# First blocks, attention and spatial gate of a streaming encoder step, with other tiles, engines and transposes

## Chip, cores and metric

One core of a Trainium2 chip runs the kernel. The metric is the device time of one execution in microseconds, the median of several runs.

## Reference

One layer of an encoder for two groups that share the weights: a prompt of 256 positions and a sample of 64 positions with 256 cached ones, 2048 features, 8 heads of 128, 8 spatial groups of 128, a feed-forward width of 5632. All in 32-bit floats. Cut to what matters:

```python
xn = rmsnorm(x, norm_mix)
q, k, v, u, vs, g = split(xn @ w_in)
# attention, for each head and query, keys in order:
z = (q . k) * 128 ** -0.5
mask = k_pos < q_pos
log_stay = where(mask, log_sigmoid(-z), 0)
log_rest = cumsum(log_stay, reverse=True) - log_stay
w = where(mask, exp(log_sigmoid(z) + log_rest), 0)
a = w @ v                       # sample: cached keys and values ahead of the new ones
# spatial gate, chunks of 128 positions, 8 groups:
vs = rmsnorm(gelu(vs), sgu_norm)
bb = gelu(u) * (w_spatial_masked @ vs + b_spatial)
h = x + (g_a * (a @ w_branch_a) + g_b * (bb @ w_branch_b)) @ w_out   # g_a, g_b: sigmoids of g
h = h + (silu(hn @ w_gate) * (hn @ w_up)) @ w_down                   # hn = rmsnorm(h)
y = rmsnorm(h)                  # and the new k, v and vs rows
```

## The kernel before

Features lie on partitions and the 320 positions of both groups side by side on the free axis. A 32-bit product is made of three matmuls in the reduced format fp32r: weight and activation are each split in a high and a low part, and `product` (lines 77 to 82) issues high x high (L80), high x low (L81), low x high (L82), each 128x128 by 320 columns. `block` (L84) makes one output block of 128 features from 16 k-chunks in two halves of 8. For each half `weights` (L67) lets the SP queue load 512 KB into one of three `raw` buffers, ScalarE cast it to `wh` (L72) and VectorE subtract to get `wl` (L73); four split buffers exist. Behind each half `tick` (L61) runs the steps that `at` has put at that count. A half is 24 matmuls.

The first stage computes q, k and v of heads 0 and 1 in six accumulators at once, two k-chunks a step, loads of x and weights alternating on the SP queue. Its norm `rms` (L156: one matmul by ones, square root, reciprocal, a Newton step) follows; behind one half `first_out` scales the six accumulators (L369, L372). Then heads 2 to 7 follow, three blocks each.

Attention goes by pairs of heads: `att_scores` (keys on rows; the sample's queries in strips), softplus by Abs, Exp, Ln on ScalarE and a sum on VectorE (L301 to L304), a split in two parts (L305, L306), `att_sums` (twelve matmuls by triangular and full matrices of -1, L317 to L322), `turned` (transposes of V on TensorE, L334) and `att_out` for each head (L357 to L360). `attend` (L381) sets their places: 2, 4, 6, 9 and 10 halves behind a pair's end. The spatial gate works the same way group by group (`sgu_turn`, `sgu_mix`, L419 to L436) between the blocks of u. Each engine runs its own instructions in program order, so a cast or a subtraction of weights waits for what stands ahead of it in its engine's queue. The ScalarE functions Exp and Ln need their tables loaded at each change between them.

## Time and profile before

| | |
|---|---|
| runs (us) | 1741.28, 1743.64, 1743.3; median 1743.3 |
| span of the profiled execution (us) | 1739.3 |
| TensorE (PE) busy | 1719.8 us, 99%, 11,672 instructions |
| VectorE (DVE) busy | 857.6 us, 49% |
| ScalarE (ACT) busy | 677.3 us, 39% |
| GpSimd (POOL) busy | 55.8 us, 3% |
| DMA | 263.20 MB, mean 151 GB/s |
| granted TensorE clock | 0.994 of full speed on average |

The span runs from the first to the last instruction of one profiled execution; the timed runs contain a little more around it. Busy shares are averages over the whole span. The chain that ended last lies on TensorE for 96% of the span, on the three lines of `product` for 31% each. A matmul's row gives its start and how long it was in the array; consecutive matmuls overlap, so the distance of starts tells what one costs.

### The profile page before, as it was taken

To read this page: it belongs to the slowest core of one execution; us is meant where nothing else is said; L and a number is where in the kernel's file an instruction comes from. 1 tells how busy PE (TensorE), PEld (TensorE's weight loads), DVE (VectorE), ACT (ScalarE), POOL (GpSimd) and SP (SyncE) were. 2 spreads that over 40 slices of the span, in tenths; PEclk is the share of its full clock that TensorE was granted. 3 is DMA by queue.
4 is the path that set the end of the run, shared out by engine and by line. 5 is a ranking of instruction groups with operands and counts; after the bars stand their busy time and mean duration, and the time that the engine had idled before them with its cause. 6 is when DMAs were issued, how large, how long until landed. Compare 5 with 4: busy or idle time off the path is not lost.

```text
span 1739.3 us, 27593 instructions
## 1 busy us (share of the span) xinstructions
PE 1719.8 (99%) x11672; PEld 1711.9 (98%) x11672; DVE 857.6 (49%) x1089; ACT 677.3 (39%) x832; POOL 55.8 (3%) x94
## 2 busy tenths in 40 slices
PE   9999999999999999999999999999999999999997
PEld 9999999999999999999999999999999999999996
DVE  6554446554444444555444444444444444444455
ACT  6554475333333333444333333233333323333342
POOL 1100001000000000220000000000000000000000
PEclk9999999999999999999999999999999999999998
DMA  7644434344444444554444444444444444444453
GB/s 215 200 155 161 142 119 151 122 146 147 154 148 148 155 146 155 175 172 149 154 146 149 154 146 150 153 145 151 152 147 152 150 148 153 148 148 153 129 152 109
DMA packets 80172, 263.20 MB, mean 151 GB/s; under 512 B 9008, under 2 KB 16432, under 8 KB 80048
## 3 DMA queue, kind: packets, MB, share of 16 engines
q1 hardware_dynamic: 77184, 252.74, 44.8%
q0 software_dynamic: 2720, 8.65, 1.5%
q8 instruction: 91, 1.49, 0.3%
q14 instruction: 33, 0.27, 0.0%
q10 hardware_dynamic: 144, 0.05, 0.0%
HBM read 255.90 MB, written 5.51 MB: 150 GB/s over the span
## 4 chain that ended last, share of the span: by engine, by line
PE 96%; DMA 2%; DVE 1%; ACT 1%; issue 0%; SPq 0%; DVEq 0%; ACTq 0%
PE acc L82 31%; PE acc L81 31%; PE acc L80 31%; DMA raw<-w_in 1%; ACT wh L72 0%; DVE wl L73 0%; PE aux L357 0%; DVE h L541 0%; DMA x<-xT 0%; PE aux L285 0%; PE aux L334 0%; PE aux L359 0%; PE aux L281 0%; PE aux L430 0%; PE aux L429 0%
## 5 line engine op out<-in xcount | busy, mean ns | idle before, releaser
L72 ACT CAST wh<-raw 128x1024 fp32r<-128x1024 f32 (+2 forms) x486 | 498.1, 1025 | 991.1 <-PE acc L81 802.1
L73 DVE TENSOR_TENSOR wl<-raw,wh 128x1024 fp32r<-128x1024 f32 (+2 forms) x486 | 580.6, 1195 | 527.7 <-ACT wh L72 527.3
L80 PE MATMUL acc<-A,wh 128*128 128x320 f32 x2496 | 775.6, 311 | 5.4 <-DVE q L369 3.4
L82 PE MATMUL acc<-A,wl 128*128 128x320 f32 x2496 | 772.7, 310 | 0.0
L81 PE MATMUL acc<-A,wh 128*128 128x320 f32 x2496 | 772.5, 309 | 0.0
L80 PEld LDWEIGHTS acc<-A,wh 128*128 128x128 f32 x2496 | 469.5, 188 | 6.5 <-issue 3.6
L82 PEld LDWEIGHTS acc<-A,wl 128*128 128x128 f32 x2496 | 469.6, 188 | 0.6 <-DVE wl L73 0.5
L81 PEld LDWEIGHTS acc<-A,wh 128*128 128x128 f32 x2496 | 469.7, 188 | 0.2
L82 PE MATMUL acc<-B,wl 128*128 128x320 f32 x960 | 296.6, 309 | 0.0
L80 PE MATMUL acc<-B,wh 128*128 128x320 f32 x960 | 296.6, 309 | 0.0
L81 PE MATMUL acc<-B,wh 128*128 128x320 f32 x960 | 296.6, 309 | 0.0
L80 PEld LDWEIGHTS acc<-B,wh 128*128 128x128 f32 x960 | 180.2, 188 | 0.0
L81 PEld LDWEIGHTS acc<-B,wh 128*128 128x128 f32 x960 | 180.2, 188 | 0.0
L82 PEld LDWEIGHTS acc<-B,wl 128*128 128x128 f32 x960 | 180.2, 188 | 0.0
L80 PE MATMUL acc<-mh,wh 128*128 128x320 f32 x256 | 79.1, 309 | 0.0
L81 PE MATMUL acc<-ml,wh 128*128 128x320 f32 x256 | 79.1, 309 | 0.0
L82 PE MATMUL acc<-mh,wl 128*128 128x320 f32 x256 | 79.1, 309 | 0.0
L503 DVE TENSOR_TENSOR bb<-acc,rh 128x320 f32<-128x320 f32 x44 | 21.6, 491 | 57.8 <-PE acc L82 57.8
L500 DVE TENSOR_TENSOR ev<-acc,rh 128x320 f32<-128x320 f32 x44 | 21.6, 491 | 56.6 <-PE acc L82 56.6
L513 DVE TENSOR_TENSOR h<-acc,h 128x320 f32<-128x320 f32 x48 | 23.5, 489 | 49.9 <-PE acc L82 49.9
L80 PEld LDWEIGHTS acc<-mh,wh 128*128 128x128 f32 x256 | 48.1, 188 | 0.0
L81 PEld LDWEIGHTS acc<-ml,wh 128*128 128x128 f32 x256 | 48.1, 188 | 0.0
(200 smaller groups left out, 761.2 us busy)
## 6 DMA issues: line engine op xcount, KB each, us to landing
raw<-w_gu SPq DMA_DIRECT2D x176, 512.0 KB, 3.5
raw<-w_in SPq DMA_DIRECT2D x132, 512.0 KB, 3.6
raw<-w_down SPq DMA_DIRECT2D x80, 512.0 KB, 3.5
raw<-w_out SPq DMA_DIRECT2D x32, 512.0 KB, 3.6
raw<-w_a SPq DMA_DIRECT2D x16, 512.0 KB, 3.5
raw<-w_b SPq DMA_DIRECT2D x16, 512.0 KB, 3.5
raw<-w_in SPq DMA_DIRECT2D x14, 384.0 KB, 5.0
raw<-w_down SPq DMA_DIRECT2D x16, 256.0 KB, 2.7
```

Of the source, the lines that this page charges most:

```text
L72: nc.scalar.copy(out=wh[:, : n * P], in_=raw[:, : n * P])
L73: nc.vector.tensor_tensor(out=wl[:, : n * P], in0=raw[:, : n * P], in1=wh[:, : n * P].bitcast(F32), op=ALU.subtract)
L80: nc.tensor.matmul(ps[:, :T], a, x[0], start=first, stop=False)
L81: nc.tensor.matmul(ps[:, :T], a, x[1], start=False, stop=False)
L82: nc.tensor.matmul(ps[:, :T], b, x[0], start=False, stop=last)
L500: nc.vector.tensor_tensor(out=t, in0=pg, in1=got["rh"], op=ALU.mult)
L503: nc.vector.tensor_tensor(out=u, in0=pu, in1=got["rh"], op=ALU.mult)
L513: nc.vector.tensor_tensor(out=hs[m], in0=ps, in1=hs[m], op=ALU.add)
```

## The change

First stage: ten raw buffers of its own (`raw1`), x loaded by pairs of chunks and some pairs ahead (`ahead`), squares by pairs; the norm's matmul stands before the last step's products; the six accumulators are scaled at once behind the stage. Attention: the two heads of a pair are handled together, queries on rows. The sample's queries of both heads share a tile (`qs`, 64 columns a head), and the products with cached keys and values fill 64 of 128 output rows each. The reverse cumulative sum is a scan on VectorE, five a pair (L311). The weights, V and the gate's input are transposed as two 16-bit planes: ScalarE copies a plane (L266, L267, L323), a transposing DMA on ScalarE's queue turns it (L269, L324), VectorE copies it back into 32-bit words (L277, L331). `att_out` makes both heads' prompt rows, and the sample's rows are transposed on TensorE from a copy (`own`). The spatial gate goes by pairs of groups, with a block-diagonal matrix `wd` for the sample. The activations' pairs of tiles come from one pool of 24 (before: 8 and a second pool). Nine warming matmuls instead of eight. The three lines of `product` are L82 to L84 now, cast and subtraction L69 and L70. A cut of the diff; lines taken out are seen in the functions above:

```diff
+    steps = [(0, 1), (1, 1)] + [(c, 2) for c in range(2, KD, 2)]
+    ahead = {0: (0,), 1: (1,), 2: (2,), 3: (3, 4), 4: (5, 6), 5: (7,)}
+    NS = len(steps)
+    xp, xs, squares = {}, [], []
...
+    rpool = raw_ctx.enter_context(tc.tile_pool(name="first", bufs=1))
...
+    def load_x(i):
+        xp[i] = pair("x")
+        nc.sync.dma_start(out=xp[i], in_=xT[:, 2 * i : 2 * i + 2, :])
+
+    def load_w(h, c, n):
+        raw = rpool.tile([P, 6 * P], F32, tag="raw1", bufs=10, name="raw1")
+        nc.sync.dma_start(out=raw[:, : 3 * n * P].rearrange("p (b k) -> p b k", b=3),
+                          in_=w_qkv[h, :, :, c * P : (c + n) * P])
+        return raw
...
+        for s, (c, n) in enumerate(steps):
+            raws = [load_w(0, c, n)]
+            for i in ahead.get(s + 1, ()):
+                load_x(i)
+            raws.append(load_w(1, c, n))
             ws = []
...
+                ws.append(halved(raws[h], 3 * n))
+                if h == 0:
+                    for m in range(c, c + n):
+                        xs.append(gained(xp[m // 2][:, m % 2, :], g_mix[:, m : m + 1]))
+            if s == NS - 1:
+                nc.vector.tensor_tensor(out=totx, in0=squares[0][:, 0, :], in1=squares[0][:, 1, :], op=ALU.add)
+                got["rx"] = rms("rx", totx, D)
...
+            if 1 <= s < NS - 1:
+                square(s - 1)
+            if s == NS - 2:
+                square(7)
+    raw_ctx.close()
...
+    mask = apool.tile([P, 4, P], F32, name="mask")
+    nc.gpsimd.memset(mask, 0.0)
+    for i in (0, 2, 3):
+        nc.gpsimd.affine_select(out=mask[:, i, :], in_=mask[:, i, :], pattern=[[-1, P]], base=0,
...
+    attn[0] = {}
+    att_load(0)
...
+    def mix_load():
+        nc.gpsimd.dma_start(out=wst.rearrange("p g t -> p (g t)"), in_=ws_t)
+        nc.gpsimd.memset(wst[64:128, :, 0:64], 0.0)
+        nc.gpsimd.dma_start(out=bsb.rearrange("p g t -> p (g t)"), in_=bs.to_broadcast([P, H * P]))
+        nc.gpsimd.memset(wd, 0.0)
...
+            nc.gpsimd.dma_start(out=wd[64 * j : 64 * j + 64, :, 64 * j : 64 * j + 64],
+                                in_=by[0:64, :, j, 0:64])
...
+    def turn_begin(t2):
+        hw = t2.bitcast(U16).rearrange("p j (t w) -> p j t w", w=2)
+        flat = pair("flat", (2, 5 * P), U16)
+        for i in range(2):
+            nc.scalar.copy(out=flat[:, i, 0:512].rearrange("p (j t) -> p j t", j=2), in_=hw[:, :, 0:TP, 1 - i])
+            nc.scalar.copy(out=flat[:, i, 512:640].rearrange("p (j t) -> p j t", j=2), in_=hw[:, :, TP:T, 1 - i])
+        turned = pair("turned", (2, 5, P), U16)
+        nc.scalar.dma_start_transpose(out=turned.rearrange("p i b d -> p (i b) d"),
+                                      in_=flat.rearrange("p i t -> p (i t)"))
+        return turned
...
+        hw = rows.rearrange("p b d -> p (b d)").bitcast(U16).rearrange("p (n w) -> p n w", w=2)
+        for i in range(2):
+            nc.vector.tensor_copy(hw[:, :, 1 - i], turned[:, i].rearrange("p b d -> p (b d)"))
+        return rows
...
+        q, k, ck = s["q"], s["k"], s["ck"]
+        zb, zc = [aux(), aux()], aux()
+        for j in range(2):
+            nc.tensor.matmul(zb[j][:, 0:128], q[:, j, 0:128], k[:, j, 0:128], start=True, stop=True)
+            nc.tensor.matmul(zb[j][:, 128:384], q[:, j, 128:256], k[:, j, 0:256], start=True, stop=True)
+        nc.tensor.matmul(zc[:, 256:384], s["qs"], k[:, :, TP:T], start=True, stop=True)
+        for j in range(2):
+            nc.tensor.matmul(zc[64 * j : 64 * j + 64, 0:256], s["qs"][:, 64 * j : 64 * j + 64], ck[:, j, :], start=True, stop=True)
...
+        for j in range(2):
+            nc.vector.tensor_tensor(out=w[:, j * 384 : (j + 1) * 384], in0=zb[j][:, 0:384], in1=flat[:, 0:384], op=ALU.add)
+        nc.scalar.copy(out=w[:, 768:1024], in_=zc[:, 0:256])
+        nc.vector.tensor_tensor(out=w[:, 1024:NA], in0=zc[:, 256:384], in1=flat[:, 384:512], op=ALU.add)
+        for r in (slice(0, 768), slice(768, NA)):
+            nc.scalar.activation(out=e[:, r], in_=w[:, r], func=AF.Abs)
+            nc.scalar.activation(out=e[:, r], in_=e[:, r], func=AF.Exp, scale=-1.0)
+            nc.scalar.activation(out=e[:, r], in_=e[:, r], func=AF.Ln, bias=1.0)
 
...
+        w, e = s["w"], s["e"]
+        c = s["c"] = apool.tile([P, NA], F32, tag="c", name="c")
+        for r in (slice(0, 768), slice(768, NA)):
+            nc.vector.scalar_tensor_tensor(out=e[:, r], in0=w[:, r], scalar=0.0, in1=e[:, r], op0=ALU.max, op1=ALU.add)
+            for a, b in SEGMENTS:
+                if r.start <= a < r.stop:
+                    back = slice(b - 1, a - 1 if a else None, -1)
+                    nc.vector.tensor_tensor_scan(out=c[:, back], data0=e[:, back], data1=e[:, back],
+                                                 initial=0.0, op0=ALU.add, op1=ALU.max)
+            nc.vector.tensor_tensor(out=w[:, r], in0=w[:, r], in1=c[:, r], op=ALU.subtract)
+
+    def att_weights(p):
+        s = attn[p]
+        w = s["w"]
+        nc.scalar.activation(out=w, in_=w, func=AF.Exp)
+        hw = w.bitcast(U16).rearrange("p (n w) -> p n w", w=2)
+        flat = s["e"].bitcast(U16).rearrange("p (i n) -> p i n", i=2)
+        to = s["c"].bitcast(U16).rearrange("p (i n) -> p i n", i=2)
+        for i in range(2):
+            nc.scalar.copy(out=flat[:, i, :], in_=hw[:, :, 1 - i])
+            nc.scalar.dma_start_transpose(out=to[:, i, :].rearrange("p (b q) -> p b q", q=P), in_=flat[:, i, :])
...
+        for i in range(2):
+            nc.vector.tensor_copy(hw[:, :, 1 - i], to[:, i, :])
+        s["vn"] = turn_end(s["turned"])
...
     def att_values(p):
+        attn[p]["turned"] = turn_begin(attn[p]["v"])
...
+        wt, vn, cvt = s["w"].rearrange("p (b q) -> p b q", q=P), s["vn"], s["cv"]
+        so, po = aux(), aux()
+        for i in range(2):
+            for j in range(2):
+                nc.tensor.matmul(so[64 * j : 64 * j + 64, 0:P], wt[:, 6 + i, 64 * j : 64 * j + 64],
+                                 cvt[:, i, j, :], start=i == 0, stop=False, skip_group_check=True)
+        nc.tensor.matmul(so[:, 0:P], wt[:, 8, :], vn[:, 4, :], start=False, stop=True, skip_group_check=True)
+        own = tmp.tile([P, P], F32, tag="own", bufs=1, name="own")
+        nc.scalar.copy(out=own, in_=so[:, 0:P])
...
+            nc.tensor.matmul(po[:, j * 256 : (j + 1) * 256], vn[:, 2 * j, :],
+                             wt[:, 3 * j : 3 * j + 2, :], start=True, stop=False)
+            nc.tensor.matmul(po[:, j * 256 + 128 : (j + 1) * 256], vn[:, 2 * j + 1, :],
+                             wt[:, 3 * j + 2, :], start=False, stop=True)
+        nc.tensor.transpose(so[:, P : 2 * P], own, ident)
...
+        for src, r in ((po, slice(0, TP)), (so[:, P : 2 * P], slice(TP, T))):
+            v = src.rearrange("p (j t) -> p j t", j=2)
+            nc.scalar.copy(out=hi[:, :, r], in_=v)
+            nc.vector.tensor_tensor(out=lo[:, :, r], in0=v, in1=hi[:, :, r].bitcast(F32), op=ALU.subtract)
...
+            if h % 2:
+                s["qs"] = tmp.tile([P, P], F32, tag="qs", bufs=1, name="qs")
+                nc.scalar.copy(out=s["qs"].rearrange("p (j t) -> p j t", j=2), in_=s["q"][:, :, TP:T])
...
     def attend(p, now):
-        at(now + 2, att_scores, p)
-        at(now + 4, att_values, p)
-        at(now + 6, att_sums, p)
-        at(now + 9, att_out, p, 0)
-        at(now + 10, att_out, p, 1)
-
-    got["rx"] = rms("rx", [totx], D)
-    attn[0] = {}
-    at(state["tick"] + 1, first_out)
-    at(state["tick"] + 1, att_load, 0)
-    attend(0, state["tick"] + 2)
+        at(now + 1, att_scores, p)
+        at(now + 1, att_values, p)
+        at(now + 2, att_sums, p)
+        at(now + 3, att_weights, p)
+        at(now + 5, att_join, p)
+        at(now + 8, att_out, p)
+
+    for name, b in (("q", 0), ("k", 1), ("v", 2)):
+        for h in range(2):
+            head_out(name, first[h][b][:, :T], h)
+    at(state["tick"] + 4, mix_load)
+    attend(0, state["tick"] + 1)
...
+        vn = turns.pop(p)
+        pg, pd = aux(), aux()
+        for j in range(2):
+            for c in range(2):
+                at0 = (2 * j + c) * P
+                nc.tensor.matmul(pg[:, at0 : at0 + P], vn[:, 2 * j + c, :], wst[:, 2 * p + j, :], start=True, stop=True)
+        nc.tensor.matmul(pd[:, 0:P], vn[:, 4, :], wd[:, p, :], start=True, stop=True)
...
     base = state["tick"]
     at(base + 1, sgu_norm)
-    for g in range(H):
-        at(base + 2 + 2 * g, sgu_turn, g)
-        at(base + 4 + 2 * g, sgu_mix, g)
+    for p in range(H // 2):
+        at(base + 3 + 4 * p, sgu_turn, p)
+        at(base + 5 + 4 * p, sgu_join, p)
+        at(base + 6 + 4 * p, sgu_mix, p)
```

TensorE at the end of the first stage, before: the norm's matmul (L160, of the sum of squares `totx`) stands between the last product of the stage and the first block of head 2.

```order
L82 MATMUL aux<-A,wl 128x320
L160 MATMUL aux_635<-totx,ones 128x320
L80 MATMUL acc<-A,wh 128x320
L81 MATMUL acc<-A,wh 128x320
L82 MATMUL acc<-A,wl 128x320
```

After, the place ahead of the stage's last step:

```order
L83 MATMUL aux<-A,wh 128x320
L84 MATMUL aux<-A,wl 128x320
L134 MATMUL aux_572<-totx,ones 128x320
L82 MATMUL acc<-A,wh 128x320
L83 MATMUL acc<-A,wh 128x320
L84 MATMUL acc<-A,wl 128x320
```

The norm's matmul (L134 now) moved ahead of the last step's 36 products, and the block of head 2 follows the stage without it.

ScalarE in the first pair, before, from the split of the softplus (L305) over V's copies from the accumulators (L338) to the weights' Exp (L325, L328):

```order
L305 CAST sph<-e 128x512
L303 ACT_TABLE_LOAD
L303 ACTIVATE e<-e 128x640
L338 COPY vn<-aux 128x384 x2
L72 CAST wh<-raw 128x1024
L305 CAST sph<-e 128x640
L72 CAST wh<-raw 128x1024 x2
L325 ACT_TABLE_LOAD
L325 ACTIVATE zm_807<-zm_807 128x512
L328 ACTIVATE zm_808<-zm_808 128x640
```

After, in the first pair, from the Ln of the softplus's first part (L300) over the weights' Exp (L318) to the transposing DMAs:

```order
L300 ACTIVATE e<-e 128x768
L299 ACT_TABLE_LOAD
L299 ACTIVATE e<-e 128x384
L69 CAST wh<-raw 128x1024
L300 ACT_TABLE_LOAD
L300 ACTIVATE e<-e 128x384
L69 CAST wh<-raw 128x1024
L318 ACT_TABLE_LOAD
L318 ACTIVATE w<-w 128x1152
L323 COPY e<-w 128x1152 x2
L324 DMA_TRANSPOSE c<-e 128x9x128 x2
L69 CAST wh<-raw 128x1024 x5
```

Ahead of the weights' Exp the two parts change tables four times, with one cast of weights (L69) between; behind the Exp two copies of 1152 elements and two transposing DMAs stand ahead of the next five casts.

VectorE in the second pair, before: the sums' results (L324 to L327) are added to the scores between two subtractions of weights (L73):

```order
L73 TENSOR_TENSOR wl<-raw,wh 128x1024
L324 TENSOR_TENSOR zm_1221<-aux,zm_1221 128x512
L326 TENSOR_TENSOR zm_1222<-aux,zm_1222 128x256
L327 TENSOR_TENSOR zm_1222<-aux,zm_1222 128x384
L73 TENSOR_TENSOR wl<-raw,wh 128x1024
L372 TENSOR_TENSOR k<-acc,rx 128x320
L73 TENSOR_TENSOR wl<-raw,wh 128x1024 x2
L115 TENSOR_TENSOR B<-aux_1508,B 128x320
L369 SCALAR_TENSOR_TENSOR q<-acc,rx 128x320
L73 TENSOR_TENSOR wl<-raw,wh 128x1024
```

After, in the second pair, from the last scan (L311) to the joins:

```order
L311 SCALAR_TENSOR_TENSOR c<-e 128x384
L313 TENSOR_TENSOR w<-w,c 128x768
L313 TENSOR_TENSOR w<-w,c 128x384
L70 TENSOR_TENSOR wl<-raw,wh 128x1024 x2
L371 SCALAR_TENSOR_TENSOR q<-acc,rx 128x320
L277 COPY rows<-turned 128x640 x2
L331 COPY w<-c 128x1152
L70 TENSOR_TENSOR wl<-raw,wh 128x1024
L331 COPY w<-c 128x1152
L70 TENSOR_TENSOR wl<-raw,wh 128x1024
```

The subtractions of weights (L70) stand behind the scans and between the two joins (L331), each of which needs a transposing DMA's data, and behind V's joins (L277).

## Rows read from the trace of the kernel before

**Rows 1.** page, part 1: busy us of each engine (share), instructions.
```profile
PE 1719.8 (99%) x11672; PEld 1711.9 (98%) x11672; DVE 857.6 (49%) x1089; ACT 677.3 (39%) x832; POOL 55.8 (3%) x94
```

**Rows 2.** stretches: us, busy us (instructions) by engine, PEclk, DMA share, GB/s.
```profile
12.00:14.00 2.00, 0.59 (x2) 0.59 (x3) 0.61 (x1) 1.23 (x2) 0.00 (x0) 0.87 0.96 274
64.70:68.00 3.30, 3.30 (x14) 3.30 (x14) 1.81 (x3) 0.00 (x0) 2.06 (x4) 0.50 0.78 267
1000.00:1400.00 400.00, 400.00 (x2729) 400.00 (x2728) 182.63 (x207) 133.75 (x149) 0.00 (x0) 1.00 0.47 150
```

**Rows 3.** waits of PE: instruction, what it waited for, us, times, longest.
```profile
PE acc L80 <- DVE q L369: 3.4, 1, 3.4
PE acc L80 <- ACT wh L72: 2.0, 2, 1.7
```

**Rows 4.** PE's timeline, a pair's scores: start, us, engine, line, operation, count.
```profile
115.47 0.59 PE L281 MATMUL aux<-q,k 128*128 128x256 f32 x2
115.91 0.38 PE L282 MATMUL aux<-q,k 128*128 128x128 f32 x2
116.12 0.61 PE L285 MATMUL aux<-q,ck 128*128 128x128 f32 x4
...
118.04 0.39 PE L80 MATMUL acc<-A,wh 128*128 128x320 f32 x1
```

**Rows 5.** PE's timeline, V's transposes of a pair.
```profile
81.47 0.82 PE L334 MATMUL aux<-ident,v 128*128 128x128 f32 x6
82.04 0.39 PE L80 MATMUL acc<-A,wh 128*128 128x320 f32 x1
```

**Rows 6.** PE's timeline, sums: first of twelve, and the product behind.
```profile
89.17 0.40 PE L317 MATMUL aux<-sph,negtr 128*128 128x512 f32 x1
...
90.93 0.31 PE L80 MATMUL acc<-A,wh 128*128 128x320 f32 x1
```

**Rows 7.** PE's timeline, out of one head.
```profile
101.49 0.60 PE L357 MATMUL aux<-zm,cv 128*128 128x128 f32 x4
102.02 0.48 PE L357 MATMUL aux<-zm,vn 64*128 64x128 f32 x2
102.44 0.70 PE L359 MATMUL aux<-zm,vn 128*128 128x256 f32 x2
...
103.11 0.39 PE L80 MATMUL acc<-A,wh 128*128 128x320 f32 x1
```

**Rows 8.** PE's timeline, a mix with the next turn.
```profile
290.00 0.49 PE L429 MATMUL aux<-wst,vn 64*128 64x128 f32 x2
...
291.21 0.39 PE L80 MATMUL acc<-A,wh 128*128 128x320 f32 x1
```

**Rows 9.** VectorE's timeline, behind the first stage.
```profile
57.73 2.15 DVE L151 RECIPROCAL rx<-rx 128x320 f32<-128x320 f32 x1 [0.62 <-ACT rx L165]
...
62.51 0.89 DVE L369 SCALAR_TENSOR_TENSOR q<-acc,rx 128x320 f32<-128x320 f32 x2
```

**Rows 10.** ScalarE's groups by shape, 50 to 360 us: count, busy, mean ns, idle.
```profile
L72 ACT CAST wh<-raw 128x1024 fp32r<-128x1024 f32 x75 | 78.3, 1047 | 119.9 <-PE acc L81 109.0 <-DMA raw<-w_in 7.9 <-PE acc L82 3.0
L303 ACT ACT_TABLE_LOAD x8 | 10.3, 1283 | 0.1
...
L305 ACT CAST sph<-e 128x640 fp32r<-128x640 f32 x4 | 2.9, 732 | 0.0
```

**Rows 11.** VectorE's groups by shape, 50 to 360 us.
```profile
L73 DVE TENSOR_TENSOR wl<-raw,wh 128x1024 fp32r<-128x1024 f32 x75 | 92.2, 1229 | 79.8 <-ACT wh L72 79.7
...
L304 DVE SCALAR_TENSOR_TENSOR e<-zm,e 128x640 f32<-128x640 f32 x4 | 3.3, 826 | 3.2 <-ACT e L303 3.2
```

**Rows 12.** DMA view: transfer, queue, count, KB each, median us to landing.
```profile
raw<-w_down SPq DMA_DIRECT2D x16, 256.0 KB, 2.7
...
bsb<-bs POOLq DMA_DIRECT2D x1, 512.0 KB, 10.3
```

**Rows 13.** timeline of the start: a DMA's issue on ScalarE's queue.
```profile
0.82 0.41 ACTq L130 DMA_DIRECT2D gain<-gains  x1
```

More of the change, by code (lines that the diff above doesn't have):

```diff
@@ L28 @@
 QSCALE = 128.0 ** -0.5
-WARM = 8
+WARM = 9
 @with_exitstack
@@ L64, in tick, with halved @@
             fn(*a)
-    def weights(src, n, view=lambda t: t):
-        raw = wraw.tile([P, HALF * P], F32, tag="raw", name="raw")
-        nc.sync.dma_start(out=view(raw[:, : n * P]), in_=src)
+    def halved(raw, n):
         wh = wsplit.tile([P, HALF * P], F32R, tag="wh", name="wh")
@@ L75, in weights @@
         return wh, wl
+    def weights(src, n):
+        raw = wraw.tile([P, HALF * P], F32, tag="raw", name="raw")
+        nc.sync.dma_start(out=raw[:, : n * P], in_=src)
+        return halved(raw, n)
     def product(ps, w, j, x, first, last):
@@ L97, in slot, with pair, gained @@
         return big.tile([P, T], F32R, tag=tag, bufs=32, name=tag)
[L99 to L119 removed]
+    def pair(name, shape=(2, T), dt=F32):
+        return big.tile([P, *shape], dt, tag="D", bufs=24, name=name)
+    def gained(src, gain):
+        hi, lo = slot("A"), slot("A")
         nc.scalar.activation(out=hi, in_=src, func=AF.Copy, scale=gain)
@@ L154, in newton, with rms @@
         nc.vector.scalar_tensor_tensor(out=r, in0=e, scalar=1.5, in1=r, op0=ALU.add, op1=ALU.mult)
-    def rms(name, totals, width):
+    def rms(name, total, width):
         ps = aux1()
-        for i, t in enumerate(totals):
-            nc.tensor.matmul(ps[:, :T], ones, t, start=i == 0, stop=i == len(totals) - 1)
+        nc.tensor.matmul(ps[:, :T], ones, total, start=True, stop=True)
         ms = t320("ev")
@@ L403, in stream_step, with half @@
     sq = Squares("sq_v")
-    vs, _ = halves(H, "vs")
+    vs, us = [], []
+    def half(tiles, g, name):
+        if g % 2 == 0:
+            tiles.append(pair(name))
+        return tiles[g // 2][:, g % 2, :]
     for g in range(H):
@@ L426, in sgu_mix @@
-    def sgu_mix(g):
-        vn = vnat.pop(g)
-        pg = aux()
-        nc.tensor.matmul(pg[:, 256:384], vn[:TS, 2, :], wst[:TS, g, :], start=True, stop=True)
-        nc.tensor.matmul(pg[:, 0:128], vn[:, 0, :], wst[:, g, :], start=True, stop=True)
-        nc.tensor.matmul(pg[:, 128:256], vn[:, 1, :], wst[:, g, :], start=True, stop=True)
-        b = t320("bb")
-        for lo, n in ((0, 128), (128, 128), (256, 64)):
-            nc.vector.tensor_tensor(out=b[:, lo : lo + n], in0=pg[:, lo : lo + n], in1=bsb[:, g, 0:n], op=ALU.add)
-        nc.vector.tensor_tensor(out=b, in0=b, in1=us[g], op=ALU.mult)
-        bT[g] = split("B", b)
+        v = half(vs, g, "vs")
@@ new lines, in stream_step, with sgu_turn @@
+        nc.scalar.activation(out=v, in_=t, func=AF.Gelu_apprx_tanh)
+        sq.add(v)
+    bT: list = []
+    turns = {}
+    def sgu_norm():
+        got["rv"] = rms("rv", sq.total, H * P)
+    def sgu_turn(p):
+        for j in range(2):
+            g, v = 2 * p + j, vs[p][:, j, :]
+            nc.vector.scalar_tensor_tensor(out=v, in0=v, scalar=g_sgu[:, g : g + 1], in1=got["rv"],
+                                           op0=ALU.mult, op1=ALU.mult)
+            nc.gpsimd.dma_start(out=sv_t[g], in_=v[:, TP:T])
+        turns[p] = turn_begin(vs[p])
@@ L504, in finish @@
             nc.vector.tensor_tensor(out=u, in0=u, in1=t, op=ALU.mult)
-            act.append(split("B", u))
+            a = pair("act", dt=F32R)
+            nc.scalar.copy(out=a[:, 0, :], in_=u)
+            nc.vector.tensor_tensor(out=a[:, 1, :], in0=u, in1=a[:, 0, :].bitcast(F32), op=ALU.subtract)
+            act.append((a[:, 0, :], a[:, 1, :]))
         for j in range(s0, s0 + n):
```

252 lines of the change are left out of this document (74 added, 178 removed).

## Prediction, made before the changed kernel was run

> **What bounds the kernel now.** I read the busy times first: TensorE is busy 1719.8 of 1739.3 us [rows 1]. So only work taken off TensorE, or a wait put on it, moves the time. The stretch 1000 to 1400 us, products alone, holds 2729 matmuls: 400/2729 = 0.1466 us each [rows 2]. The kernel issues 3776 products of three, 11,328 x 0.1466 = 1660.7 us, so 1739.3 - 1660.7 = 78.6 us are start, end, waits and the small matmuls of attention and mix. The list of waits gives the largest, 3.4 us for the first q [rows 3]; the timeline gives the small matmuls, each segment from its first start to the next product's. The scores take 115.47 to 118.04 = 2.57, four times, 10.3 [rows 4]; V's transposes 0.57, four times, 2.3 [rows 5]; the sums 89.17 to 90.93 = 1.76, four times, 7.0 [rows 6]; out 1.62, eight times (once per head), 13.0 [rows 7]; mix with a turn 1.21, seven times, 8.5, and the two ends of that pipeline about one more, 1.1 [rows 8]. Together 42.1 us (unrounded). VectorE and ScalarE are half idle, but every weight half needs one cast (1.05) and one subtraction (1.23) [rows 10, 11] within the 24 x 0.1466 = 3.52 us of a half; four split buffers are the slack.
>
> **What leaves TensorE.** New small matmuls, priced by [rows 4]: 256 columns 0.44, 128 columns 0.21 to 0.22.
> Scores per pair: 2 x (0.21 + 0.44) + 0.21 = 1.51, and two half-width ones of 256 columns, 0.88 in a row or 0.44 side by side. No row shows side by side. [rows 7] show a 64-row tile dearer: 0.42 instead of 0.21 (102.02 to 102.44). I take 0.88: 2.4; bounds 1.95 and 2.7. Sums: none, scans on VectorE stand for them.
> Out per pair: four half-width of 128 (0.84), one of 128 (0.21), two of 256 and two of 128 (1.30), a transpose 0.57/6 = 0.1 [rows 5], switching tiles 0.3: 2.7. The transpose waits for a ScalarE copy, which the 1.3 us behind it hide; uncovered it would be some 0.4 (a copy of 128 elements and its way there).
> Mix per pair: five of 0.21 to 0.22 = 1.08. All transposes of V and of the SGU leave.
>
> 6.18 x 4 = 24.7 us (21.5 to 27.5) stand for 42.1: a gain of 17.4 (14.6 to 20.6).
>
> **First blocks.** "rx" now stands 36 products, 36 x 3 x 0.1466 = 15.8 us, ahead of the stage's end. From the reciprocal at 57.73 to q at 62.51 the chain takes 4.8 us [rows 9], which leaves 11.0 for its matmul, square root and first eviction, more than they need: it is hidden, and the 3.4 us go. What is late next is the eviction of six accumulators (three times 0.89 = 2.7, [rows 9]); a third accumulator buffer lets the next block start under it, so I expect no further wait. TensorE ran at half clock just behind this wait: 14 matmuls in 3.3 us at a granted 0.50, where 2.05 were due: 1.3 back [rows 2]. A gain of 4.7.
> The raw buffers take away a wait for splits at the start, 2.0 us for casts [rows 3], but all x in pairs puts about 640 KiB more ahead of the second half's last weights, 2.4 us at the 274 GB/s of that time [rows 2]. Between -1 and +3.3 I take +1.5. Total gain 23.6.
>
> **What the change can make wait.** TensorE no longer computes the sums, but the next weights' cast and subtraction stand in ScalarE's and VectorE's queues behind attention's steps. S is the scores' start.
> Pair 0: on ScalarE the weights of the half in question wait behind V's copies (1.9), the transposing DMA's issue X, two casts (2.1), the copy from PSUM (0.4), Abs, Exp and Ln over 768 and 384 elements (3 x 1.36, by the slope between [rows 10]'s 640 and 1024) and four table loads (4 x 1.28): 13.6 + X. Then VectorE needs the tail: sum, scan, subtraction, two joins, q and wl = 6.0 [rows 11]. The half is ready at S - 0.6 + 13.6 + X + 6.0 = S + 19.0 + X. TensorE wants it after the scores and four halves: S + 2.4 + 14.1 = S + 16.5. The issue of a DMA on ScalarE's queue took 0.41 [rows 13]; a transposing one has ten blocks to describe, so X is 0.4 to 3 and I take 1.5. Stall 4.0 (2.9 to 5.5).
> Pairs 1 and 2: the first transposing DMA of W is issued at about S + 17.7 by the same sums. VectorE waits for it, copies 1152 elements (1.36) and only then subtracts a half (1.23) due at S + 2.4 + 6 x 3.52 = S + 23.5. Its landing L has no row: plain transfers of 256 KB took 2.7, the slow broadcast of bsb 10.3 [rows 12]. I take 4, nearer to the plain one, as 288 KB in SBUF are a plain transfer's size: S + 17.7 + 4 + 2.6 = 24.3, 0.8 late, twice 0.8. At 2.7 nothing is late.
> Pair 3, with GELU's table among it: 1.5, by the mean of the others (0 to 4).
> A stall can drop the clock as in [rows 2]; two stretches, 2.6.
> POOL's queue: wst, bsb and the small diagonal loads now stand there with k's and v's stores behind them; nobody waits for the stores within a stage, and ck and cv of the next pair are issued some eight halves (28 us) ahead of their use. I take nothing; if bsb's 10.3 [rows 12] held ck back beyond that, a loss of a few us once.
>
> Scans: 1152 elements in five instructions cost 2.0 by [rows 11]'s slope (1.05 ns an element, 0.15 fixed); a reciprocal's 2.15 for 320 is the dear end, 7 us a pair. I take the first, an addition being its nearest kind. [...] No row before shows a scan.
>
> **Sum.** Losses 4.0 + 0.3 (rounding of the half's end) + 1.6 + 1.5 + 2.6 = 10.0. Net -13.6. The profiled span, 1739.3, lies 4.0 below the median 1743.3; what lies around it doesn't change. 1739.3 - 13.6 + 4.0 = 1730.
>
> **Rivals.**
> First, the transposing DMAs are slow (slower than before). If each takes bsb's 10.3 us and they run one behind the other, the first of W lands at S + 28.0, its half is ready at 30.6, 7.1 late; the second lands 10.3 later with one half (3.52) between: 6.8 more. 13.9 a pair, three times, and 17 in pair 0, where V's stands ahead; the four of the SGU leave 6.4 us between turn and join, 3.9 late each; half clock behind eight of the stalls, 8 x 1.3. Together 41.7 + 17 + 15.6 + 10.4 = 85, net +61: 1804. The point from which it decides is L of about 6.3, where the stalls reach 23.6. For it speaks that 2-byte elements are moved to other partitions, against it that bsb was one broadcast row with many readers and its neighbours were busy. [...] Chance 0.20.
> Second, the queues fit (faster still). L is 2.7 or less, X 0.4, and only pair 0's 2.9 and one half-clock 1.3 remain; with half-width products side by side 3 more: 23.6 + 3 - 4.2 = 22 to 28 gained, 1715 to 1721. Chance 0.15.
> Third, the stalls eat the gain: L near 6, X near 3. Pair 0 5.5, the others 4 each, clock 5: about 22 lost, 1742. Chance 0.10.
> That the change doesn't take the small matmuls off TensorE as it says is no rival of its own: the order shows them gone, and half-width products at their dear end are +1.2, inside the forecast.
>
> **Chances and range.** The forecast (1722 to 1738) 0.55, rivals 0.20, 0.15, 0.10. A difference of 0.2%, 3.5 us, is about what a measurement of this kernel can tell from no change. Faster than 1739.8: 0.55 + 0.15 = 0.70; within: 0.10; slower: 0.20. The range reaches down to 1713 and up to 1765, which holds the milder third of rival 1 (L up to 8) and leaves out its rest.
>
> **What would show it.** Right: no wait for q behind rx; matmuls of attention and mix about 25 us in all; the longest TensorE waits on the subtraction of one half in pair 0 (about 4) and small ones in pairs 1 to 3; transposing DMAs landing in 3 to 5 us. Wrong: VectorE idle for a transposing DMA over 6 us in front of a join, TensorE waits of 5 us and more for wl in every pair, granted clock 0.5 behind them; or weight transfers that take over 5 us beside transposing ones, which this sum leaves out; or a scan over 3 us a pair.

## The result, and the profile after

The changed kernel takes 1747.5 us (median of 7 runs, 1743.0 to 1754.1) where the kernel before takes 1743.2 beside it (7 runs, 1741.3 to 1744.1): a ratio of 1.0033, 95% interval 1.0018 to 1.0048. It is slower by 0.3%. The forecast of 1730 had the wrong sign, though 1747.5 lies inside its range. The profiled execution spans 1747.8 us, 8.5 more than that of before.

The page's busy times and chain, to set beside [rows 1]:

```profile
PE 1705.2 (98%) x11542; PEld 1696.4 (97%) x11542; DVE 868.8 (50%) x1079; ACT 675.9 (39%) x837; POOL 57.4 (3%) x93
...
PE 90%; DMA 3%; ACT 3%; DVE 2%; issue 1%; ACTq 1%; SPq 0%; DVEq 0%
```

TensorE is busy 14.6 us less, and the span is longer all the same. Its chain share fell to 90%: DMA, ScalarE and VectorE stand in it now. The waits of TensorE (what waited, for what, us in all, times, longest), to set beside [rows 3]:

```profile
PE aux L353 <- ACT own L347: 13.5, 4, 4.8
PE acc L84 <- DVE wl L70: 11.3, 4, 5.4
PE acc L82 <- ACT wh L69: 3.7, 5, 1.0
```

The wait for q is gone. In its place stand 28.5 us: four waits of the transpose in `att_out` for its copy `own`, four waits for a subtraction of weights and five for a cast. Four of the five casts' waits, 2.7 us, lie in the first 17 us, where the kernel before waits 2.0 for casts; the other 25.8 us lie in attention. Behind five of the longer waits the granted clock drops to half, as in [rows 2]. Two of the five stretches (length, TensorE busy and instructions, ..., granted clock, DMA share, GB/s):

```profile
80.20:83.20 3.00, 3.00 (x13) 3.00 (x13) 1.10 (x2) 1.04 (x1) 0.57 (x1) 0.50 0.80 159
104.10:107.20 3.10, 3.10 (x13) 3.10 (x14) 1.71 (x3) 0.57 (x2) 0.00 (x0) 0.50 0.38 118
```

They hold 13 instructions in 3.0 to 3.1 us; in their timeline two starts of products lie 0.27 us apart instead of 0.1466. Summed over the slow steps, the five stretches cost 7.8 us.

Where the time went, by stage: I summed, from TensorE's timeline, every distance of two starts beyond 0.1466 us a product matmul.

| beyond products, us | before | after | difference |
|---|---|---|---|
| first stage, norm and the wait for q | 14.2 | 8.7 | -5.5 |
| pair 0 | 8.5 | 22.0 | +13.5 |
| pair 1 | 8.5 | 8.4 | -0.1 |
| pair 2 | 8.5 | 12.5 | +4.0 |
| pair 3 | 8.8 | 12.2 | +3.4 |
| spatial gate | 11.7 | 5.0 | -6.7 |
| the rest | 6.4 | 6.4 | 0 |

The small matmuls of a pair, with the way back to the products, take 4.8 us now (scores 2.2, out with its transpose 2.2, the rest is the way back); the pairs without a wait in the runs below show the same 4.8. So about 36 us of the four pairs' 55.1 are waits, half clock and the restart behind each wait. The gains are about 27: 5.5 in the first stage, and 22 in attention and gate, which fell from 46.0 (before, all of these rows) to 24.1 without the waits (4 x 4.8 and 5.0).

How one pair loses it, in pair 1. ScalarE's timeline (start, length, engine, line, operation, idle before and what ended it; "ACTq" rows are its DMA issues):

```profile
135.44 5.48 ACTq L324 DMA_TRANSPOSE c<-e  x2
141.02 2.95 ACT L69 CAST wh<-raw 128x1024 fp32r<-128x1024 f32 x3 [4.56 <-issue]
147.88 1.04 ACT L69 CAST wh<-raw 128x1024 fp32r<-128x1024 f32 x1 [3.92 <-DMA raw<-w_in]
151.27 1.04 ACT L69 CAST wh<-raw 128x1024 fp32r<-128x1024 f32 x1 [2.35 <-DMA raw<-w_in]
152.22 0.26 ACT L347 COPY own<-aux 128x128 f32<-128x128 f32 x1
```

VectorE's in the same stretch:

```profile
135.61 0.95 DVE L277 COPY rows<-turned 128x640 uint16<-128x640 uint16 x2
142.08 0.85 DVE L331 COPY w<-c 128x1152 uint16<-128x1152 uint16 x1 [5.52 <-ACT wh L69]
142.82 1.20 DVE L70 TENSOR_TENSOR wl<-raw,wh 128x1024 fp32r<-128x1024 f32 x1
```

W's two transposing DMAs hold ScalarE's queue from 135.44 to 140.92. VectorE stands in front of the first join (L331) with its queue closed for 5.5 us, until 142.08. (The row names a cast as what ended it, whose end falls on the same tenth; the first transfer, issued at 135.44, landed, that is, had all its data in place, 6.5 us later, at 141.94, by the DMA view, where columns are count and us to landing.)

```profile
c<-e ACTq DMA_TRANSPOSE x1, 6.5
```

Only behind it is the next half subtracted (142.82), and only then are its raw buffers free. SP's next loads go out at 144.05 (SP's timeline):

```profile
144.05 6.49 SPq L76 DMA_DIRECT2D raw<-w_in  x4
```

The casts of 147.88 and 151.27 wait for them ("DMA raw<-w_in", 3.92 and 2.35). `own` is queued behind that cast: 152.22. TensorE stands in front of the transpose meanwhile:

```profile
152.53 0.33 PE L353 MATMUL aux<-ident,own 128*128 128x128 f32 x1 [2.66 <-ACT own L347]
```

The same place in pair 0, on TensorE's timeline:

```profile
98.80 0.66 PE L343 MATMUL aux<-cv,w 128*64 128x128 f32 x8
99.39 0.49 PE L345 MATMUL aux<-rows,w 128*128 128x128 f32 x2
...
103.97 0.47 PE L353 MATMUL aux<-ident,own 128*128 128x128 f32 x1 [2.79 <-ACT own L347]
```

The prompt's four matmuls end at 101.2; the transpose (L353) starts at 103.97, after 2.79 us of idle time.

### The profile page after: what moved, and what is told of

It reads as the page before. It is cut to its first block, busy times and chain, and to the rows that moved or that the text cites. A ratio compares the mean times of both kernels' runs of the same rounds, so it can differ in the third digit from the quotient of the medians.

```text
span 1747.8 us, 27345 instructions
## 1 busy us (share of the span) xinstructions
PE 1705.2 (98%) x11542; PEld 1696.4 (97%) x11542; DVE 868.8 (50%) x1079; ACT 675.9 (39%) x837; POOL 57.4 (3%) x93
## 4 chain that ended last, share of the span: by engine, by line
PE 90%; DMA 3%; ACT 3%; DVE 2%; issue 1%; ACTq 1%; SPq 0%; DVEq 0%
PE acc L82 29%; PE acc L84 29%; PE acc L83 29%; DMA raw<-w_in 2%; DMA c<-e 2%; ACT wh L69 1%; PE aux L82 0%; PE aux L83 0%; PE aux L84 0%; DVE wl L70 0%; ACTq L269 0%; ACT e L323 0%; DVE c L311 0%; DVE h L560 0%; ACTq L324 0%
## 5 line engine op out<-in xcount | busy, mean ns | idle before, releaser
L69 ACT CAST wh<-raw 128x1024 fp32r<-128x1024 f32 (+2 forms) x486 | 497.7, 1025 | 1004.3 <-PE acc L83 766.2
L70 DVE TENSOR_TENSOR wl<-raw,wh 128x1024 fp32r<-128x1024 f32 (+2 forms) x486 | 580.0, 1195 | 504.0 <-ACT wh L69 503.4
L84 PE MATMUL acc<-A,wl 128*128 128x320 f32 x2496 | 775.5, 311 | 11.3 <-DVE wl L70 11.3
L82 PE MATMUL acc<-A,wh 128*128 128x320 f32 x2496 | 777.1, 311 | 3.7 <-ACT wh L69 3.7
L84 PEld LDWEIGHTS acc<-A,wl 128*128 128x128 f32 x2496 | 471.5, 189 | 12.7 <-DVE wl L70 12.5
L82 PEld LDWEIGHTS acc<-A,wh 128*128 128x128 f32 x2496 | 472.1, 189 | 6.7 <-ACT wh L69 4.9
L84 PE MATMUL acc<-act,wl 128*128 128x320 f32 x704 | 217.5, 309 | 0.0
L82 PE MATMUL acc<-act,wh 128*128 128x320 f32 x704 | 217.5, 309 | 0.0
L83 PE MATMUL acc<-act,wh 128*128 128x320 f32 x704 | 217.5, 309 | 0.0
L82 PEld LDWEIGHTS acc<-act,wh 128*128 128x128 f32 x704 | 132.1, 188 | 0.0
L83 PEld LDWEIGHTS acc<-act,wh 128*128 128x128 f32 x704 | 132.1, 188 | 0.0
L84 PEld LDWEIGHTS acc<-act,wl 128*128 128x128 f32 x704 | 132.1, 188 | 0.0
L82 PE MATMUL acc<-mh,wh 128*128 128x320 f32 x256 | 79.1, 309 | 0.0
L84 PE MATMUL acc<-mh,wl 128*128 128x320 f32 x256 | 79.1, 309 | 0.0
L82 PEld LDWEIGHTS acc<-mh,wh 128*128 128x128 f32 x256 | 48.0, 188 | 0.0
```

The lines of the kernel that those rows point to most:

```text
L69: nc.scalar.copy(out=wh[:, : n * P], in_=raw[:, : n * P])
L70: nc.vector.tensor_tensor(out=wl[:, : n * P], in0=raw[:, : n * P], in1=wh[:, : n * P].bitcast(F32), op=ALU.subtract)
L82: nc.tensor.matmul(ps[:, :T], a, x[0], start=first, stop=False)
L83: nc.tensor.matmul(ps[:, :T], a, x[1], start=False, stop=False)
L84: nc.tensor.matmul(ps[:, :T], b, x[0], start=False, stop=last)
```

## Experiments

Each is timed against the kernel before on the same chip; what a pair "spends" is its microseconds beyond products in the profiled execution, as in the table, from its scores to the next pair's.

### The transpose of own, one half later

```diff
-        nc.tensor.transpose(so[:, P : 2 * P], own, ident)      # in att_out, at now + 8
+    def att_last(p):                                           # at now + 9
+        nc.tensor.transpose(so[:, P : 2 * P], own, ident)
...
```

> The transpose of own and the two copies behind it stand one half later; nothing else moves. Theory (the copy own is late because it stands in ScalarE's queue behind a cast that waits for weights, and TensorE stands in front of the transpose): the four waits for own, 13.5 us, go, and 0 to 4 us come back as waits for casts of weights: 1734 to 1738. Rival (the weights behind are late in any case, so that TensorE only waits somewhere else): the waits for L69 and L70 grow by what own loses, 1745 to 1749.

Measured: 1734.2 us (1731.5 to 1736.9); ratio 0.9958, interval 0.9941 to 0.9975. TensorE's waits:

```profile
PE acc L84 <- DVE wl L70: 12.7, 4, 5.8
PE acc L82 <- ACT wh L69: 1.9, 3, 1.0
...
PE aux L358 <- ACT own L348: 0.5, 1, 0.5
```

The wait for `own` fell to 0.5, and the wait for subtractions grew by only 1.4: 13.3 us for moving this transpose and the copies behind it. The step alone turns the change from slower to faster. The pairs spend 19.8, 4.8, 7.3 and 5.7 us now; what is left are mainly the waits for subtractions, 10 us of them in pair 0.

### Which transposing DMAs: V, W, or all

V's back to TensorE:

```diff
-        attn[p]["turned"] = turn_begin(attn[p]["v"])
+        attn[p]["vown"] = turn_own(attn[p]["v"])       # a copy of the samples' columns
+    def att_turn(p):                                   # at now + 4: five transposes, two copies
+        attn[p]["vn"] = turn_pe(attn[p]["v"], attn[p]["vown"])
```

> Attention's V is transposed on TensorE again (five transposes a pair, two copies on ScalarE); the weights W and the gate keep the transposing DMAs. Theory (ScalarE is held for 4.2 us by the issue of V's transposing DMA, which makes pair 0 late): the first wait of pair 0, 4.1 us, and part of its second go, TensorE gets 0.5 us a pair more; the waits for own in pairs 1 to 3 stay: 1740 to 1745. Rival (the landing of W's transposing DMAs sets all of it): pair 0 still waits 9 us, 1747 to 1750.

Measured: 1742.2 us; ratio 0.9995, interval 0.9984 to 1.0006.

```profile
PE aux L362 <- issue: 8.9, 2, 7.9
PE aux L372 <- ACT own L366: 6.4, 3, 4.1
```

Pair 0's first wait for a subtraction went, but 7.9 us came back in front of `att_out`'s first product (L362), which needs the joined W: pair 0 spends 16.1 us instead of 22.0. V's transposing DMA is a part of pair 0's loss; the larger part stays with W. How much of that part is V's issue is not shown: with it gone, ScalarE also loads three tables in pair 0 up to the weights' Exp instead of five.

W to TensorE, V's stay:

```diff
-            nc.scalar.copy(out=flat[:, i, :], in_=hw[:, :, 1 - i])
-            nc.scalar.dma_start_transpose(out=to[:, i, :]..., in_=flat[:, i, :])
-            nc.vector.tensor_copy(hw[:, :, 1 - i], to[:, i, :])
+            for b in range(0, n, P):                   # at now + 6, three groups of 4, 4 and 1
+                nc.tensor.transpose(pt[:, b : b + P], w[:, lo + b : lo + b + P], ident)
+            move(out=c[:, lo : lo + n], in_=pt[:, 0:n])
```

> The attention weights W are transposed on TensorE (nine transposes a pair, three copies), V and the gate keep the transposing DMAs. Theory (VectorE waits for W's transposing DMAs at the joins, so the raw weight buffers come free late, their loads and casts are late, and own is late behind the casts): waits for own fall from 13.5 to under 4 us, those for L70 from 11.3 to about 5 (pair 0's V), TensorE gets 0.9 us a pair more: 1728 to 1734. Rival (own is late by its place behind a cast, whatever the DMAs do): waits for own stay over 10 us, 1738 to 1745.

Measured: 1720.1 us (1719.5 to 1722.0); ratio 0.9873, interval 0.9858 to 0.9888. All waits on weights that are left (`own` has none):

```profile
PE acc L82 <- ACT wh L69: 2.9, 4, 1.2
PE acc L84 <- DVE wl L70: 1.9, 1, 1.9
```

The casts' waits lie in the first stage. It went further than I expected. Nine transposes cost TensorE 0.90 us a pair, 3.6 in all, and 27.4 us are won net, so some 31 us of waits and half clock go. `own` was late only because the casts ahead of it were late.

No transposing DMA at all: both edits above, and the gate's input on TensorE.

```diff
-        turns[p] = turn_begin(vs[p])
+        turns[p] = turn_own(vs[p])
...
-        turns[p] = turn_end(turns[p])
+        turns[p] = turn_pe(vs[p], turns[p])
```

> No transposing DMA at all: V, W and the gate's input are transposed on TensorE; pairs, scans, half-width products and the first blocks stay. Theory (all losses hang on the transposing DMAs): only waits of own of some 0.5 us a pair are left; small matmuls 5.7 us a pair and 1.5 a gate pair: 1721 to 1728. Rival (pairs and scans make the queues late by themselves): waits of 8 us and more stay, 1732 to 1740.

Measured: 1721.4 us; ratio 0.9879, interval 0.9864 to 0.9893. One wait line on weights, again in the first stage:

```profile
PE acc L82 <- ACT wh L69: 1.8, 3, 0.9
```

Pairs, scans and half-width products make no queue late by themselves. Against the run before it nothing more is won: V's five transposes cost 0.55 us a pair and save pair 0's wait of 1.9, and the gate's cost 2.2 in all, where its DMAs had cost no wait (the gate spends 7.2 instead of 5.0).

### The transposing, or a transfer at that place

```diff
-            nc.scalar.dma_start_transpose(out=to[:, i, :].rearrange(...), in_=flat[:, i, :])
+            nc.scalar.dma_start(out=to[:, i, :], in_=flat[:, i, :])
```

> W's two DMAs on ScalarE's queue copy the 288 KB without transposing (the transposition of the attention weights is left out); copies, joins, orders and all else stay. Theory (it is the transposing that is dear, in the time its issue holds ScalarE and in its landing): the issue takes 0.4 us, landing 3 to 4, waits for own under 2 us, only pair 0's wait behind V's transposing DMA (some 2 to 4) stays: 1720 to 1728. Rival (any transfer of this size at this place makes VectorE's joins and the raw loads late): waits for own over 8 us, 1736 to 1747.

Measured: 1739.0 us (1735.7 to 1743.1); ratio 0.9984, interval 0.9971 to 0.9996. My theory missed by over 10 us, and its rival was right:

```profile
PE aux L353 <- ACT own L347: 10.4, 4, 3.1
```

The DMA queues' issues in pair 1, and the join on VectorE:

```profile
126.34 1.46 SPq L76 DMA_DIRECT2D raw<-w_in  x2
...
127.60 1.53 ACTq L324 DMA_DIRECT2D c<-e  x2
```

```profile
135.01 0.83 DVE L331 COPY w<-c 128x1152 uint16<-128x1152 uint16 x1 [6.29 <-DMA c<-e]
```

Two plain issues span 1.53 us where two transposing ones spanned 5.48, yet the first landed 7.3 us after its issue (DMA view), and its join starts at 135.01: no sooner than the transposing one of this pair (6.5). Two loads of weights of 512 KB had been issued just ahead, at 126.34 and 127.48. Over the four pairs the eight plain transfers landed in 6.7 us by the median and the transposing ones in 7.5, of which pair 0's two took 11.8 and 10.8 and the others 5.8 to 7.8. So the transposing is not the main part of the late landing outside pair 0, and VectorE's 6.29 us in front of the join remain. The theory had to be split in two: ScalarE held by the issues, and VectorE closed in front of the join.

### V's transposing DMA twice

```diff
+            spare = pair("spare", (2, 5, P), U16)
+            nc.scalar.dma_start_transpose(out=spare..., in_=flat...)
```

> Attention's V is sent through a transposing DMA twice, the second into a spare tile that nobody reads. Theory (the issue holds ScalarE, 4.2 us each, and what stands behind it on ScalarE): pair 0 waits 4 us more, pairs 1 to 3 1 to 4 us more each: 1754 to 1766. Rival (only the landing that VectorE waits for counts, and the second has no reader): 1745 to 1751.

Measured: 1758.2 us (1753.2 to 1760.0); ratio 1.0090, interval 1.0070 to 1.0111: 10.7 us more than the changed kernel, for transfers that nobody reads.

```profile
PE acc L84 <- DVE wl L70: 13.4, 6, 6.2
```

So a transfer on ScalarE's queue costs even where nothing waits for its landing, which is what holding ScalarE would do; that the second transfer also takes DMA time from the others is not separated here. The split by pairs was not as I wrote it: pair 0 did not grow (20.4 us; in the program's order a cast of weights now stands ahead of W's copies there, which may be why); pairs 1 to 3 grew by 3.8, 0.5 and 1.8 in the profiled execution, which at 1751.4 is the shortest of the runs.

### The same DMAs on SP's queue

```diff
-        nc.scalar.dma_start_transpose(...)     # V, W and the gate
+        nc.sync.dma_start_transpose(...)
```

> All transposing DMAs are issued on SP's queue, among the loads of weights, instead of ScalarE's. Theory (ScalarE held by issues): pair 0's first wait goes and the waits for own shrink to under 5 us, but weight loads stand behind the issues and casts wait for raw some 1 to 2 us a pair: 1732 to 1742. Rival (the landing at VectorE's joins sets everything, and loads behind the issues add to it): 1746 to 1756.

Measured: 1716.7 us (1716.5 to 1717.0); ratio 0.9857, interval 0.9842 to 0.9872, far below what either theory gave.

```profile
PE acc L82 <- ACT wh L69: 2.9, 4, 1.0
PE aux L353 <- ACT own L347: 1.8, 2, 1.0
...
PE acc L84 <- DVE wl L70: 1.1, 1, 1.1
```

SP's issues in pair 1, and the joins:

```profile
119.20 0.33 SPq L76 DMA_DIRECT2D raw<-w_in  x1
...
120.45 3.63 SPq L324 DMA_TRANSPOSE c<-e  x2
...
124.19 4.14 SPq L76 DMA_DIRECT2D raw<-w_in  x3
```

```profile
124.50 0.85 DVE L331 COPY w<-c 128x1152 uint16<-128x1152 uint16 x1 [0.81 <-DMA c<-e]
126.05 0.84 DVE L331 COPY w<-c 128x1152 uint16<-128x1152 uint16 x1 [0.70 <-DMA c<-e]
```

Here the loads of weights queue behind the transposing DMAs (next at 124.19) and only one 512 KB load is ahead (119.20). The first lands 4.05 us after its issue (120.45 to 124.50), the second 3.3 after 122.72, against 6.5 on ScalarE's queue with two loads in flight. VectorE stands 0.8 us in front of the joins, not 5.5. ScalarE is held by nothing. One subtraction also moved ahead of the joins in the program's order. SP's 3.6 us cost nothing that TensorE shows: the casts' 2.9 us lie in the first stage. The pairs spend 7.4, 4.8, 5.8 and 4.8 us.

### The join behind two subtractions, and both edits together

```diff
+        if p < 3:          # the join waits for the next pair's v
+            nc.gpsimd.tensor_copy(s["w"][:, 0:1], attn[p + 1]["v"][:, 0, 0:1])
-        at(now + 5, att_join, p)
-        at(now + 8, att_out, p)
+        at(now + 7 if p else now + 6, att_join, p)
+        at(now + 9, att_out, p)
```

> ScalarE's queue keeps all transposing DMAs. In pairs 1 and 2 the joins are bound to the next v, so that two subtractions of weights stand ahead of them instead of between and behind them; out comes one half later in all pairs. Pairs 0 and 3 keep their order. Theory (VectorE stands in front of the join until W's transposing DMA has landed, 6 to 7 us beside weight loads, and the raw buffers, loads, casts and own come late from that): pairs 1 and 2 lose their waits for own and casts, what TensorE spends there beyond products falls from 8.4 and 12.5 us to about 5 each; 1734 to 1740. Rival (ScalarE held by the issue makes the casts and own late): both stay at 8 us and more, 1744 to 1750.

Measured: 1735.3 us (1734.8 to 1737.5); ratio 0.9962, interval 0.9947 to 0.9977. Pairs 1 and 2 spend 5.6 and 7.2 us, pair 0 15.1, and pair 3, whose join kept its place, 13.2:

```profile
PE acc L84 <- DVE wl L70: 11.3, 5, 5.1
PE aux L355 <- ACT own L349: 3.9, 4, 1.6
```

The time is the theory's, but it does not show the joins' share: the whole of out stands one half later too, and the first experiment, which moved only out's transpose, left pairs 1 and 2 at 4.8 and 7.3. VectorE no longer waits for the landing in pair 1, yet it is closed nearly as long, now for a cast that stands behind W's issues on ScalarE (128.77 to 133.76, the cast at 133.86):

```profile
134.94 2.36 DVE L70 TENSOR_TENSOR wl<-raw,wh 128x1024 fp32r<-128x1024 f32 x2 [5.91 <-ACT wh L69]
```

Together with the plain copies (both diffs):

> Both single edits together: W's two DMAs copy without transposing (the transposition of the attention weights is left out), and in pairs 1 and 2 the joins stand behind two subtractions. Theory (two causes, ScalarE held by the issue and VectorE standing in front of the join, each enough to make casts and own late): with both gone pairs 1 and 2 spend 4.5 to 6 us beyond products each, where the first edit alone left 12.2 and 11.6; pair 3 keeps its wait; 1722 to 1728. Rival (one cause, the other edit only shifts it): pairs 1 and 2 stay at 8 us and more, 1730 to 1736.

Measured: 1723.1 us (1721.2 to 1724.0); ratio 0.9894, interval 0.9877 to 0.9910. Pairs 1 and 2 spend 4.8 us each, as the theory had it, where the plain copies alone had left 12.2 and 10.0 (not 11.6); pair 3 spends 6.3 (I had left it its wait), pair 0 12.0.

```profile
PE acc L84 <- DVE wl L70: 5.6, 3, 2.8
PE aux L355 <- ACT own L349: 2.2, 2, 1.3
```

The plain copies alone gave 8.5 us and the joins alone 12.2; both give 24.4, which is not clear of the sum by the intervals. What each does to the weights shows at the fifth cast of weights behind W's issues, counted from the pair's first score:

| fifth cast, us | pair 1 | pair 2 |
|---|---|---|
| changed kernel | 31.6 | 34.2 |
| own's transpose later | 30.9 | 33.4 |
| plain copies | 32.8 | 31.6 |
| joins behind, out later | 29.0 | 31.4 |
| both | 27.4 | 27.6 |

So two queues each close the way to the weights, and in these executions neither edit alone brings the casts forward as both do. How much of the joins' 12.2 is only that out comes one half later stays open (it also helps pair 0, 22.0 to 15.1, whose join did not move); no run has plain copies with the later out alone.

### The norm alone, in the kernel before

```diff
+            if i == len(steps) - 1:        # ahead of the last step's products
+                square(); totx = ...; rx = rms("rx", [totx], D)
```

> The kernel before with one part of the change alone: the norm's matmul and its chain ahead of the first stage's last step. Theory: the wait for q (3.4 us) and the half clock behind it (1.3) go: 1737 to 1739. Rival (the lead of 36 matmuls, 5.3 us, is shorter than the chain of about 11 us, and the eviction waits in its place): 1740 to 1743.

Measured: 1738.4 us (10 runs, 1736.4 to 1741.8); ratio 0.9980, interval 0.9971 to 0.9989: 3.9 us.

```profile
PE acc L80 <- DVE q L377: 1.6, 1, 1.6
```

1.6 of the 3.4 us stay here, where the six results are still scaled one half later. The changed kernel, which scales them at once, has no such wait. In the profiled execution the first stage with the wait for q spends 10.7 us instead of 14.2, and pair 0 loses 2.7 again, most of it (2.0) in a wait of its sums for the split of the softplus.

### A version that beats both

SP's queue for the transposing DMAs, `own`'s transpose one half later, and pair 0's V on TensorE (the one whose issue took longest, 4.2 us):

```diff
+        if p == 0:
+            attn[p]["vown"] = turn_own(attn[p]["v"])
+        else:
+            attn[p]["turned"] = turn_begin(attn[p]["v"])
...
-        nc.scalar.dma_start_transpose(...)
+        nc.sync.dma_start_transpose(...)
...
+        at(now + 9, att_last, p)
```

> The transposing DMAs on SP's queue, the transpose of own one half later, and pair 0's V on TensorE. Theory: pair 0's waits behind V (about 3 us) and the two waits for own (1.8 us) go as well, 0.5 us of transposes come: 1711 to 1714. Rival (pair 0 is late by its four table loads, whatever V does): 1715 to 1717.

Measured: 1713.3 us (1712.1 to 1714.0); ratio 0.9832, interval 0.9815 to 0.9848. Pair 0 spends 5.3 us, of which its V's transposes are 0.55, and the others 4.8 each: attention has no wait left. The waits on weights that are left lie in the first 18 us:

```profile
PE acc L82 <- ACT wh L69: 2.1, 2, 1.4
```

## Why the prediction was wrong, step by step

What bounds the kernel: right. The small matmuls: the right mechanism, and a gain forecast too low; they fell from 42.1 to 21.5 us where I had 24.7. The half-width products run partly side by side. The row of the two of 256 columns (start, length), and the next product:

```profile
60.62 0.65 PE L289 MATMUL aux<-ck,qs 128*64 128x256 f32 x4
61.20 0.42 PE L82 MATMUL acc<-A,wh 128*128 128x320 f32 x1
```

0.58 us for both, where I took 0.88; the four of 128 columns take 98.80 to 99.39, 0.15 each, where I took 0.21. No row or run shows the 0.3 that I took for switching tiles; out took 2.2 with its transpose, where I had 2.7 with that term.

The norm moved ahead: the gain came (4.7 forecast; 5.5 with the first blocks), by a working that was wrong. The order shows 36 matmul rows between the two places, and I multiplied by three again: the lead is 36 x 0.1466 = 5.3 us, not 15.8. It sufficed in the changed kernel, which scales the results at once; with the same lead and the scaling one half later, 1.6 us of the wait stayed.

First blocks: +1.5 forecast, about 0.6 measured. The stage ends at 51.96 us, with the norm's matmul inside it (0.54), instead of 52.03 without. The wait for casts that the raw buffers were to take away did not go: 2.0 us before, 2.7 now. The raw buffers let SP issue earlier, and the loads only land later, 9.1 us instead of 5.0 (DMA view: count, KB, us to landing):

```profile
raw<-w_in SPq DMA_DIRECT2D x14, 384.0 KB, 9.1
...
turned<-flat ACTq DMA_TRANSPOSE x8, 6.0
c<-e ACTq DMA_TRANSPOSE x8, 7.5
```

The forecast failed on the losses, 10.0 forecast and about 36 measured. First, the copy `own`, a term put at nothing: "which the 1.3 us behind it hide; uncovered it would be some 0.4". It measured 13.5 us. I asked what TensorE has to do behind the copy, and not what stands ahead of it in ScalarE's queue: W's issues and four or five casts of weights, the last of which wait for raw loads (two of five in pair 1, three of five in pair 0). The order that I quoted ended one row ahead of it. Putting this transpose one half later gave 13.3 us back, three times what the change lost against the kernel before (4.4).

The second step that failed is the price of a DMA on ScalarE's queue. It stands behind the waits for subtractions and casts in attention, 12.3 us where 7.4 were forecast (4.0 + 0.3 + 1.6 + 1.5), 9.4 of the 12.3 in pair 0, and it is what makes the casts ahead of `own` late: W's transposes on TensorE took both away. X was taken as 1.5, up from 0.41 by the number of its blocks, an estimate that no run shows; V's first issue held the queue 4.2 us:

```profile
58.92 4.22 ACTq L269 DMA_TRANSPOSE turned<-flat  x1
```

The later V's held it 1.3 to 2.5, W's two together 5.5 to 6.4, which I had not charged at all: X stood in the sum once. L was taken as 4, with 6.3 as the point of decision; it was 6.5 in pair 1 and 11.8 in pair 0, where VectorE's queue was closed for 10.8:

```profile
92.11 0.82 DVE L331 COPY w<-c 128x1152 uint16<-128x1152 uint16 x1 [10.81 <-DMA c<-e]
```

That is rival 1's mechanism at less than half its price. Of the signs that I had named, VectorE's wait in front of a join came (over 6 us in pairs 0, 2 and 3, 5.5 in pair 1), and waits of 5 us for wl came in pair 0 alone; the largest loss, `own`, was none of the signs. I took L near the row of a plain load; no row of before showed a transfer within SBUF beside two loads of weights. And I counted only the half behind the join as late. The release of the raw buffers, and with it the loads of the next halves, hang on the same subtraction: in pair 1 VectorE's wait of 5.5 us, which ended at 142.08, was paid a second time by the casts' waits of 3.92 and 2.35, up to 151.27.

Half clock: 2.6 taken for two stretches, about 7.8 measured over five.

Scans: I took 1.05 ns an element, the price of an addition, and they took twice that; no run shows why. Groups of VectorE by shape (count, busy, mean ns):

```profile
L311 DVE TENSOR_TENSOR_SCAN c<-e 128x256 f32<-128x256 f32 x8 | 5.3, 665 | 0.0
...
L311 DVE TENSOR_TENSOR_SCAN c<-e 128x384 f32<-128x384 f32 x4 | 3.7, 937 | 0.0
L311 DVE TENSOR_TENSOR_SCAN c<-e 128x128 f32<-128x128 f32 x8 | 3.3, 409 | 0.0
```

From 128 to 384 columns, 937 - 409 = 528 ns for 256: 2.06 ns an element. A pair's five, which overlap a little, take 2.75 us from the first start to the last end instead of 2.0. This cost little beside the rest.

Transposing by DMA against TensorE: W's nine transposes by TensorE take 0.90 us a pair, 0.1 each, and are worth 27 us. By DMA nine blocks landed in 5.8 to 11.8 us on ScalarE's queue and in 4.6 by the median on SP's, where L was taken as 4. The larger part of the price was not in the transposing, since plain copies landed nearly as late (6.7 by the median for 7.5) and SP's queue made the same DMAs cheap (1716.7 us for 1747.5); it was in the queues. The gate's transposes, which rival 1 charged with 3.9 each, cost no wait.

In sum: gains 27 us for 23.6 forecast, losses 36 for 10.0: `own` 13.5 for nothing, the other waits in attention 12.3 for 7.4, half clock 7.8 for 2.6, and the restarts behind the waits. That 1747.5 lies inside the stated range is owed to the range's width; the sign was wrong.

What stays open: how much of the time that an issue holds a queue belongs to the transposing itself and how much to the transfers that are under way. SP's issues in pair 1 took 3.6 us for two, ScalarE's 5.5, plain ones 1.53, and no run separates these parts. Nor is it separated how much of the wait for weights comes from ScalarE's hold and how much from VectorE's place, beyond that neither edit alone gives what both give. Transposing DMAs on two queues at once were not tried.
